# The last two pairs of products of a decoder's short convolution, multiplied with seven block products instead of eight

## The chip, the cores and the metric

The kernel runs on one core of one Trainium2 chip. The metric is the device time of one execution in microseconds (us); the time of a kernel is the median of its runs. PE is the matrix engine, DVE the vector engine, ACT the scalar engine, POOL the GpSimd engine, SP the queue engine that issues most transfers.

## The reference

One step of a hybrid decoder layer on 512 prompt tokens and 64 decode tokens (8 sequences of 8), all in float32, side by side as 576 columns:

```python
h = _rmsnorm(x, norm1_g) * (1.0 + sc1) + sh1
proj = h @ w_in
b_gate, c_gate, xa, q, k, v, ga, gb = jnp.split(proj, cuts, axis=-1)
u = c_gate * xa
uc, new_conv = _causal_conv(u, conv_buf, conv_w)
ya = (b_gate * uc) @ w_conv_out
o, k_state, v_state = attend(q, k, v, attn_sinks.reshape(N_KV_HEADS, GROUP))
yb = o @ w_attn_out
mixed = jax.nn.sigmoid(ga) * ya + jax.nn.sigmoid(gb) * yb
x = x + g1 * (mixed @ w_mix_out)
...
a, val = jnp.split(h2 @ w_up, 2, axis=-1)
ac, new_ffn = _causal_conv(a, ffn_buf, ffn_conv_w)
x = x + g2 * ((jax.nn.gelu(ac, approximate=False) * val) @ w_down)
```

`_causal_conv` is a depthwise convolution of width 3 along the tokens. The prompt attends within a window of 128, the decode tokens to a cache of 128 rows and to themselves; both have a learned sink in the softmax. The model width is 1024, with 16 query heads and 4 key heads of 64.

## The kernel before

Activations lie transposed: 128 channels on the partitions, the 576 tokens along the row. The width of 1024 is 8 blocks of 128, numbered k where they are summed over and m where they are produced. Float32 accuracy is reached with two numbers of a shorter format for each value, a high part (`hh`, `whi`) and a low part (`hl`, `wlo`, value less high part), and three passes of matmuls: high by high, high by low, low by high.

`product(w, xs)` is the plain form for one m: for 8 k, 3 passes and 2 column groups (256 and 320) one matmul each, 48 in all. After each k it calls `tick()`.

`pair_product` does two m at once by Strassen's method. Weights are seen as 2 by 2 blocks (two halves of k, two m), activations as 2 by 2 blocks (two halves of k, two halves of 288 columns), and seven block products of 4 k and 3 passes take the place of eight: 84 matmuls of 288 columns, a tick for each of 28 k steps. They accumulate in four banks X, Y, Z, W. After parts 1 and 3 ACT copies the bank to `p1` and `p5`; after part 2 DVE makes `u = Y - p1`, after part 4 `out_a0` takes X, after part 6 DVE makes `v = Y - p1`, then `out_b0(v, W)` and `out_b1(v, p5)`, after part 7 `out_a1(Z, u)`. Y is written in parts 2 and 6, X in 1 and 4, Z in 3 and 7. The sums and differences of weights that the parts need come from `pair_weights`: four additions on DVE and four high and low parts (A, B, C of 1024 columns, D of 512). `in_turn` deals them out as steps behind parts 0, 2, 3 and 4 of the pair ahead. The low parts of B and D are made by ACT and an accumulating transfer that POOL issues, those of A and C by DVE. `PairOperands` makes the sums of the activations: `sums` (DVE: `r`, `tw`), `high` (ACT: `th`, `nh`), `low` (DVE: `tl`, `nl`) and `n3`, four of them for the four pairs of k.

The order of the stage that is changed: keys, values and the first queries come first. Then a loop over the 8 m makes c and x by two plain products each (column blocks 1024 + 128 m and 2048 + 128 m of `w_in`), c copied by ACT (L1314), u = c times x by DVE (L1324, L1325), the state kept, and `conv` run: POOL puts the old state into u, ACT does the first tap, DVE the other two, into `y`. Behind it four pairs (`b_pair`, `B_PAIRS`) make b and multiply it by y, then eight pairs make the sigmoid gates, then the output projections follow. The four `PairOperands` of h are made in the loop's last four m (4 to 7), the first b pair's weights are loaded in m = 6, and their last steps run in m = 7.

The attention runs beside all this as a generator. `fill` sets a rate, `tick()` adds the rate at each k step of a product, and each whole number that is passed runs the generator to its next `yield`. While the prompt's 16 blocks run, the rate is 0.285 (`ATT_RATE`); the decode part then takes 0.35, and 0.2 once the b pairs begin. What is left over is run by `drain()` behind the b pairs. A decode half (q = 0, 1, four sequences each) is `decode_scores` (two transposes of caches, each followed by a copy `kTc`; the scores; the softmax) and `decode_values`; the values of q = 0 come after the scores of q = 1.

PE keeps the program's order throughout the stage; ACT and DVE keep it, for the instructions issued through `act` and `dve`, from the end of the loop on, and the attention's own instructions (`nc.vector`, `nc.scalar`) don't. The rest is ordered by a scheduler with a cost model. Working tiles share 57 slots (`A_BUFS`), raw weights have 4 buffers, split weights 5; banks of PE's results are two double banks (`mm`) and four single ones (`aux`).

Of the kernel before, what the change touches and what calls it, by code (L numbers as in the profile page):

```python
# [13 lines left out]
ALU = mybir.AluOpType  # L14
# [12 lines left out]
NF = FF // P  # L27
FCH = [(0, 8), (8, 16), (16, 22)]
LATE = 4
Q_TICKS = 12  # L30
CACHE_AT = 15, 16
UP_ADDING, FIRST_TICKS = "BD", 12
ATT_RATE, ADDING_FROM, B_PAIRS = 0.285, 3, ((0, 4), (1, 5), (2, 6), (3, 7))
B_ADDING, OUT_ADDING, MOD_RATE = "BD", "BCD", 12 / 130
EPS = 1e-6
NEG = -1e33
A_BUFS = 57
# [37 lines left out]
def step_kernel(ctx: ExitStack, tc: tile.TileContext, ins: dict, outs: list):  # L75
# [76 lines left out]
    def load_w(src, nk):  # L152

        raw = wp.tile([P, nk, P], F32, tag="raw", name=nm("raw"), bufs=W_BUFS)
        sync.dma_start(raw, src)
        return raw
# [222 lines left out]
        order = {0: "sums1 ah al", 2: "dh dl sums2", 3: "bh bl", 4: "ch cl"}  # L379
        return {at: (lambda names=names: [t[n]() for n in names.split()]) for at, names in order.items()}  # L380

    def pair_product(w, x, steps, out_a0, out_a1, out_b0, out_b1):

        X, Y, Z, W = (t[:, :HT] for t in (aux(), mmps(), mmps(), aux()))
        keep, uv = slot("p15"), slot("uv")
        p1, p5, u, v = keep[:, :HT], keep[:, HT:], uv[:, :HT], uv[:, HT:]

        def part(at, bank, wn, xn_, more=False):  # L390

            (hi, lo), xs = w[wn], x[xn_]
# [547 lines left out]
    ot = [wp.tile([P, 4, NT], F32, tag="oh", name=nm("o"), bufs=2) for _ in range(2)]  # L940

    def softmax(s, n, sinks, nsinks, w):

        nmx = sp.tile([P, n], F32, tag="nmx", name=nm("nmx"))
        for x in range(n // 2):
            nc.vector.tensor_reduce(
                out=nmx[:, 2 * x : 2 * x + 2], in_=s[x][:, :, :w], axis=AX.X, op=ALU.max, negate=True
            )
# [10 lines left out]
        nc.vector.tensor_tensor(out=den, in0=den, in1=es, op=ALU.add)  # L959
        nc.vector.reciprocal(out=den, in_=den)  # L960
        for x in range(n):
            nc.vector.tensor_scalar(
                out=s[x // 2][:, x % 2, :w], in0=s[x // 2][:, x % 2, :w],
                scalar1=den[:, x : x + 1], scalar2=None, op0=ALU.mult,
            )

    caches = {}

# [10 lines left out]
    def decode_scores(q, s, cV):  # L979
# [35 lines left out]
                    in1=S[hf][:, at : at + 256], op0=ALU.mult, op1=ALU.add,  # L1015
                )
        yield False
        softmax(s, 4, snks, nsnks, 256)
        yield False

    def decode_values(q, s, cV):
# [98 lines left out]
    def attention():  # L1120
# [3 lines left out]
        for n in range(19):  # L1124
# [14 lines left out]
                h4 = slice(4 * arg[0], 4 * arg[0] + 4)  # L1139
                softmax(scored[2], 4, snk[:, h4], nsnk[:, h4], 256 if arg[1] else P)  # L1140
            yield False
        filler[1] = 0.35
        waiting = None
        for n in range(3):
            s, more = [], []
# [138 lines left out]
        for t in (2 * n, 2 * n + 1):  # L1284
            queries(t)

    for m in range(NK):
        if m in (5, 6):
            src, dst = ((ins["cache_k_win"], nks), (ins["cache_v_win"], nvs))[m - 5]
            tc.keep_in_program_order(  # L1290
                nc.gpsimd.dma_start(
                    dst[:, 0:120, :].rearrange("b (x w) c -> b x (w c)", x=2),
                    src[0].rearrange("b w h d -> b w (h d)")[:, 8:128, :].rearrange(
                        "b (x w) c -> b x (w c)", x=2
                    ),
                )
            )
        ps = product(conv_w(1024 + m * P), h)
        if m == NK - 2:
            raws = [load_w(kpm(w_in, j * P), NK) for j in B_PAIRS[0]]  # L1300
            w_pair, steps = pair_weights(*raws, B_ADDING)
            steps = in_turn(steps)
        w = conv_w(2048 + m * P)
        if m == NK - 1:
            for n in (2, 3, 4):
                steps[n]()
        if m == 0:
# [8 lines left out]
            head(1)  # L1316
        if m == 1:
            head(3)
        if m >= NK - 4:
            ops[m - NK + 4].sums()  # L1320
            ops[m - NK + 4].high()
        ps = product(w, h)
        u = padded()
        nc.vector.tensor_tensor(out=u[:, 2:514], in0=pv(ps), in1=pv(c_sb), op=ALU.mult)  # L1324
# [7 lines left out]
        if m >= NK - 4:  # L1332
            ops[m - NK + 4].low()
        if m == NK - 2:
            steps[0]()
        ys[m] = y
    pinned += [act, dve]
# [10 lines left out]
    def b_pair(ma, mb, w, steps):  # L1348
# [21 lines left out]
        pair_product(w, made["op"], steps, a0, later(ta, ya), b0, later(tb, yb))  # L1370
        gate_in[ma], gate_in[mb] = ta, tb

    gate_in, w_next, w_pair = [None] * NK, {}, [w_pair]
    filler[1:2] = [0.2] if filler else []
    gate_cols = [c + m * P for c in (4608, 5632) for m in range(0, NK, 2)]
    cols = [(ma * P, mb * P) for ma, mb in B_PAIRS[1:]] + [(c, c + P) for c in gate_cols]
    raws = {}

    def raws_for(n):
# [4 lines left out]
    def weights_for(n):  # L1384

        raws_for(n + 1)
        w, t = pair_weights(*raws.pop(n), B_ADDING if n < len(B_PAIRS) - 1 else "")
        w_pair.append(w)
        return in_turn(t)

    raws_for(0)
    for n, (ma, mb) in enumerate(B_PAIRS):
        first = [{0: lambda: [op.n3() for op in ops]}] if n == 0 else []
        b_pair(ma, mb, w_pair.pop(0), merged(*first, weights_for(n)))
    state_out(NK, ncv_p[:], ncv_s[:])
    drain()
    fill(first_modulation(), MOD_RATE)
# [46 lines left out]

    for n in range(len(gate_cols)):
        if n + 1 < len(gate_cols):
            steps = weights_for(n + len(B_PAIRS))
        else:
            drain()
            w, t = pair_weights(*out_raws(1), OUT_ADDING)  # L1450
# [688 lines left out]
```

## Time and profile before

| what | value |
|---|---|
| median of 3 runs | 979.55 us (979.48 to 979.82) |
| the profiled execution | 980.01 us, its span 978.2 us |
| granted PE clock | 0.997 of full |
| busy: PE, DVE, ACT, POOL | 965.2, 687.2, 527.3, 157.8 us |
| moved by DMA | 149.34 MB, 153 GB/s in the mean |

The span is the time from the first to the last event of the profiled execution; the execution's own time has about 1.8 us around it. Busy PE counts matmuls, whose ends are modelled, so PE's figure says little alone; it is read together with what PE waited for. The loop over m with its two products ends at about 263.1 us of the span, the four b pairs follow to about 314 us.

### The profile page before, as it was taken

Reading aid. Unit: us, or ns where it says so; the run is one execution under the profiler, and the core shown is the slowest. Engines: PE = TensorE matmul, PEld = TensorE weight load, DVE = VectorE, ACT = ScalarE, POOL = GpSimd, SP = SyncE. Lnnn points to the kernel's source line nnn. Section 1 sums busy time; section 2 is a strip of 40 time slices with the busy share of each in tenths; the row PEclk is TensorE's granted clock in tenths of the full one; section 3 lists DMA queues with packets and bytes.
Section 4 is the critical chain, followed back from the end, with each engine's and each line's share of the span. In section 5 each row is a group of like instructions: output and inputs, shape, how many; then the busy total and the mean of one; then the engine's idle time right before and its main releaser. Section 6 shows DMA issues by size and latency. Waiting matters only on the chain.

```text
span 978.2 us, 18982 instructions
## 1 busy us (share of the span) xinstructions
PE 965.2 (99%) x7420; PEld 929.5 (95%) x7420; DVE 687.2 (70%) x1337; ACT 527.3 (54%) x960; POOL 157.8 (16%) x347
## 2 busy tenths in 40 slices
PE   7999999999999999999999999999999999999997
PEld 6799999999999889999899999999999999999996
DVE  5555875674868667897578687785558874578753
ACT  6365667664654434675234468662347742256553
POOL 2132222011222000011000041220013220022120
PEclk9999999999999999999999999999999999999998
DMA  9994345475366772468952444772457762557502
GB/s 309 308 264 125 94 100 124 110 207 148 77 132 173 246 230 83 123 139 215 373 190 85 131 110 99 161 193 84 104 136 164 167 166 65 131 127 174 130 9 98
DMA packets 183563, 149.34 MB, mean 153 GB/s; under 512 B 8007, under 2 KB 161966, under 8 KB 183186
## 3 DMA queue, kind: packets, MB, share of 16 engines
q1 hardware_dynamic: 169954, 108.83, 36.5%
q0 software_dynamic: 13088, 38.52, 19.5%
q8 instruction: 58, 0.95, 0.4%
q10 hardware_dynamic: 432, 0.79, 0.2%
q14 instruction: 31, 0.25, 0.1%
HBM read 109.17 MB, written 7.35 MB: 119 GB/s over the span
## 4 chain that ended last, share of the span: by engine, by line
PE 95%; DMA 2%; SPq 1%; issue 1%; DVE 0%; POOL 0%; POOLq 0%; DVEq 0%
PE mm L114 64%; PE aux L114 27%; PE aux L1208 2%; DMA ad<-in_w_ada 2%; PE aux L1107 1%; SPq L433 1%; DMA x<-in_x_prompt 0%; POOL r L114 0%; DVE yo L114 0%; POOLq L2135 0%; DVE wlo L114 0%; DVEq L2135 0%; DVE r L114 0%
## 5 line engine op out<-in xcount | busy, mean ns | idle before, releaser
L114 ACT ACTIVATE whi<-raw 128x1024 fp32r<-128x1024 f32 (+2 forms) x174 | 177.7, 1031 | 100.7 <-PE mm L114 45.8
L114 DVE TENSOR_TENSOR wlo<-raw,whi 128x1024 fp32r<-128x1024 f32 (+2 forms) x129 | 152.2, 1183 | 49.3 <-ACT whi L114 47.5
L114 PE MATMUL mm<-hh,whi 128*128 128x256 f32 (+2 forms) x448 | 104.4, 302 | 0.6 <-ACT hh L114 0.5
L114 POOL DMA_DIRECT2D wlo<-raw x45 | 39.4, 876 | 390.8 <-ACT wlo L114 221.2
L114 PE MATMUL mm<-hh,wlo 128*128 128x256 f32 (+2 forms) x448 | 100.7, 294 | 0.1
L114 PE MATMUL mm<-hl,whi 128*128 128x256 f32 (+2 forms) x448 | 99.4, 295 | 0.3 <-DVE hl L114 0.2
L114 PEld LDWEIGHTS mm<-hh,whi 128*128 128x128 f32 x448 | 74.7, 188 | 9.8 <-issue 7.8
L114 PE MATMUL mm<-th,whi 128*128 128x288 f32 x280 | 82.7, 295 | 0.0
L114 PE MATMUL mm<-tl,whi 128*128 128x288 f32 x280 | 82.7, 295 | 0.0
L114 PE MATMUL mm<-th,wlo 128*128 128x288 f32 x280 | 82.6, 295 | 0.0
L114 PEld LDWEIGHTS mm<-hh,wlo 128*128 128x128 f32 x448 | 76.4, 188 | 0.3 <-DVE wlo L114 0.3
L114 PEld LDWEIGHTS mm<-hl,whi 128*128 128x128 f32 x448 | 75.3, 188 | 1.0 <-DVE hl L114 1.0
L114 PE MATMUL mm<-fh,whi 128*128 128x256 f32 (+1 forms) x304 | 65.4, 296 | 0.0
L114 PE MATMUL mm<-fh,wlo 128*128 128x256 f32 (+1 forms) x304 | 65.0, 295 | 0.0
L114 PE MATMUL mm<-fl,whi 128*128 128x256 f32 (+1 forms) x304 | 64.8, 294 | 0.0
L114 DVE SCALAR_TENSOR_TENSOR x<-mm,modT,x 128x512 f32<-128x512 f32 (+1 forms) x29 | 19.6, 677 | 61.8 <-PE mm L114 61.8
L114 PEld LDWEIGHTS mm<-th,whi 128*128 128x128 f32 x280 | 52.7, 188 | 0.8 <-issue 0.8
L114 PEld LDWEIGHTS mm<-th,wlo 128*128 128x128 f32 x280 | 52.7, 188 | 0.0
L114 PEld LDWEIGHTS mm<-tl,whi 128*128 128x128 f32 x280 | 52.6, 188 | 0.0
L114 PEld LDWEIGHTS mm<-fh,whi 128*128 128x128 f32 x304 | 51.0, 188 | 0.1
L114 PEld LDWEIGHTS mm<-fl,whi 128*128 128x128 f32 x304 | 50.9, 188 | 0.0
L114 PEld LDWEIGHTS mm<-fh,wlo 128*128 128x128 f32 x304 | 50.7, 188 | 0.0
(357 smaller groups left out, 2864.4 us busy)
## 6 DMA issues: line engine op xcount, KB each, us to landing
raw<-in_w_in SPq DMA_DIRECT2D x52, 512.0 KB, 4.9
wlo<-raw POOLq DMA_DIRECT2D x45, 512.0 KB, 4.9
raw<-in_w_up SPq DMA_DIRECT2D x44, 512.0 KB, 3.9
ada<-in_w_ada SPq DMA_DIRECT2D x64, 256.0 KB, 5.1
ad<-in_w_ada SPq DMA_DIRECT2D x32, 256.0 KB, 5.8
raw<-in_w_down SPq DMA_DIRECT2D x16, 512.0 KB, 4.0
wl<-s POOLq DMA_DIRECT2D x25, 256.0 KB, 4.2
raw<-in_w_conv_out SPq DMA_DIRECT2D x8, 512.0 KB, 4.5
```

Source lines behind the costliest of these rows:

```text
L114: done = getattr(self.engine, name)(*args, **kwargs)
L433: return tc.keep_in_program_order(queue.dma_start(dst, src))
L1107: done = nc.tensor.matmul(O[HALF[par], :256], vt(i - nkt + 1 + kt)[:, hd * 64 : hd * 64 + 64], pts[kt][:, par * 256 : par * 256 + 256], st ...
L1208: done = nc.tensor.matmul(ps[32 * j : 32 * j + 32, :], cT[:, k, :], cols[k][j], start=(k == 1), stop=(k == NK - 2),)
```

## The change

c and x of m = 6 and 7 are made as two Strassen pairs, c in the place of the pair's first output and x in that of its second (`cx_pair`), between the loop, which now has six m (`CX = 6`), and the b pairs. The pair's `u` of the convolution is put together in halves: ACT copies c's first half, DVE makes x's and c's others and multiplies; POOL multiplies the decode columns. W takes the second half of Y's double bank (`single=1`), so the pair holds one `aux` bank and not two. Everything tied to the loop's end comes two m sooner: h's pair operands at m = 2 to 5, the loads and weights of the first pair at m = 4 and 5. The two cache copies in DRAM are issued at m = 4 and 5, where they were at 5 and 6. The weights of both new pairs use the accumulating form for B and D, as those of the b pairs do. The decode attention runs at 0.2 from its start and has two more steps in each half, between the exponentials and the division.

```diff
+CX = 6
-ATT_RATE, ADDING_FROM, B_PAIRS = 0.285, 3, ((0, 4), (1, 5), (2, 6), (3, 7))
-B_ADDING, OUT_ADDING, MOD_RATE = "BD", "BCD", 12 / 130
+ATT_RATE, ADDING_FROM, B_PAIRS = 0.285, 3, ((0, 4), (1, 5), (2, 6), (3, 7))
+CX_RATE, B_ADDING, OUT_ADDING, MOD_RATE = 0.2, "BD", "BCD", 12 / 130
...
-    def pair_product(w, x, steps, out_a0, out_a1, out_b0, out_b1):
+    def pair_product(w, x, steps, out_a0, out_a1, out_b0, out_b1, single=2):
-        X, Y, Z, W = (t[:, :HT] for t in (aux(), mmps(), mmps(), aux()))
+        X, yw, Z = aux(), mmps(), mmps()
+        W = aux() if single == 2 else yw[:, 512:]
+        X, Y, Z, W = (t[:, :HT] for t in (X, yw, Z, W))
...
-        softmax(s, 4, snks, nsnks, 256)
+        divide = softmax_exps(s, 4, snks, nsnks, 256)
+        yield False
+        yield False
+        divide()
         yield False
...
-        filler[1] = 0.35
+        filler[1] = CX_RATE
...
-    for m in range(NK):
-        if m in (5, 6):
-            src, dst = ((ins["cache_k_win"], nks), (ins["cache_v_win"], nvs))[m - 5]
+    cx_cols = [(1024 + m * P, 2048 + m * P) for m in range(CX, NK)]
+    for m in range(CX):
+        if m in (4, 5):
+            src, dst = ((ins["cache_k_win"], nks), (ins["cache_v_win"], nvs))[m - 4]
...
-        if m == NK - 2:
-            raws = [load_w(kpm(w_in, j * P), NK) for j in B_PAIRS[0]]
+        if m == CX - 2:
+            raws = [load_w(kpm(w_in, c), NK) for c in cx_cols[0]]
             w_pair, steps = pair_weights(*raws, B_ADDING)
             steps = in_turn(steps)
...
-        if m >= NK - 4:
-            ops[m - NK + 4].sums()
-            ops[m - NK + 4].high()
+        if m >= CX - 4:
+            ops[m - CX + 4].sums()
+            ops[m - CX + 4].high()
...
+    def cx_pair(m, w, steps):
+
+        c_sb, x_sb, u, n = slot("c"), slot("x"), padded(), 512 - HT
+        done = {}
+
+        def a0(ps):
+            act.copy(c_sb[:, :HT], ps)
+
+        def b0(x, y, op):
+            dve.tensor_tensor(out=x_sb[:, :HT], in0=x, in1=y, op=op)
+            dve.tensor_tensor(out=u[:, 2 : 2 + HT], in0=x_sb[:, :HT], in1=c_sb[:, :HT], op=ALU.mult)
+
+        def b1(x, y, op):
+            dve.tensor_tensor(out=x_sb[:, HT:], in0=x, in1=y, op=op)
+
+        def a1(x, y, op):
+            c = c_sb[:, HT:]
+            dve.tensor_tensor(out=c, in0=x, in1=y, op=op)
+            dve.tensor_tensor(out=u[:, 2 + HT : 514], in0=x_sb[:, HT:512], in1=c[:, :n], op=ALU.mult)
+            nc.gpsimd.tensor_tensor(
+                out=b10(u)[:, :, 2:10], in0=b8(sv(x_sb)), in1=b8(sv(c_sb)), op=ALU.mult
+            )
+
+        pair_product(w, made["op"], steps, a0, a1, b0, b1, 1)
+        keep_state(u, m)
+        ys[m] = conv(u, parT[:, 64 + m : 65 + m], parT[:, 72 + m : 73 + m], parT[:, 80 + m : 81 + m], stT[:, m, :])
...
-    cols = [(ma * P, mb * P) for ma, mb in B_PAIRS[1:]] + [(c, c + P) for c in gate_cols]
+    cols = cx_cols[1:] + [(ma * P, mb * P) for ma, mb in B_PAIRS] + [(c, c + P) for c in gate_cols]
...
     raws_for(0)
+    for n, m in enumerate(range(CX, NK)):
+        first = [{0: lambda: [op.n3() for op in ops]}] if n == 0 else []
+        cx_pair(m, w_pair.pop(0), merged(*first, weights_for(n)))
     for n, (ma, mb) in enumerate(B_PAIRS):
-        first = [{0: lambda: [op.n3() for op in ops]}] if n == 0 else []
-        b_pair(ma, mb, w_pair.pop(0), merged(*first, weights_for(n)))
+        b_pair(ma, mb, w_pair.pop(0), weights_for(n + len(cx_cols)))
```

More of the change, by code (lines that the diff above doesn't have):

```diff
@@ L942, in softmax, with softmax_exps @@
     def softmax(s, n, sinks, nsinks, w):
+        softmax_exps(s, n, sinks, nsinks, w)()
+    def softmax_exps(s, n, sinks, nsinks, w):
         nmx = sp.tile([P, n], F32, tag="nmx", name=nm("nmx"))
@@ L958, in softmax, with divide @@
         nc.scalar.activation(es, es, AF.Exp)
[L959 to L965, printed above, removed]
+        def divide():
+            nc.vector.tensor_tensor(out=den, in0=den, in1=es, op=ALU.add)
+            nc.vector.reciprocal(out=den, in_=den)
+            for x in range(n):
+                nc.vector.tensor_scalar(
+                    out=s[x // 2][:, x % 2, :w], in0=s[x // 2][:, x % 2, :w],
+                    scalar1=den[:, x : x + 1], scalar2=None, op0=ALU.mult,
+                )
+        return divide
     caches = {}
@@ L1303, in step_kernel @@
         w = conv_w(2048 + m * P)
-        if m == NK - 1:
+        if m == CX - 1:
             for n in (2, 3, 4):
@@ L1331, in step_kernel @@
             head(2)
-        if m >= NK - 4:
-            ops[m - NK + 4].low()
-        if m == NK - 2:
+        if m >= CX - 4:
+            ops[m - CX + 4].low()
+        if m == CX - 2:
             steps[0]()
@@ L1371, in b_pair @@
         gate_in[ma], gate_in[mb] = ta, tb
+    def cx_pair(m, w, steps):
[14 more added lines that the diff above has]
+                out=b10(u)[:, :, 2:10], in0=b8(sv(x_sb)), in1=b8(sv(c_sb)), op=ALU.mult
+            )
+        pair_product(w, made["op"], steps, a0, a1, b0, b1, 1)
+        keep_state(u, m)
+        ys[m] = conv(u, parT[:, 64 + m : 65 + m], parT[:, 72 + m : 73 + m], parT[:, 80 + m : 81 + m], stT[:, m, :])
     gate_in, w_next, w_pair = [None] * NK, {}, [w_pair]
-    filler[1:2] = [0.2] if filler else []
+    filler[1:2] = [CX_RATE] if filler else []
     gate_cols = [c + m * P for c in (4608, 5632) for m in range(0, NK, 2)]
-    cols = [(ma * P, mb * P) for ma, mb in B_PAIRS[1:]] + [(c, c + P) for c in gate_cols]
+    cols = cx_cols[1:] + [(ma * P, mb * P) for ma, mb in B_PAIRS] + [(c, c + P) for c in gate_cols]
     raws = {}
@@ L1386, in weights_for @@
         raws_for(n + 1)
-        w, t = pair_weights(*raws.pop(n), B_ADDING if n < len(B_PAIRS) - 1 else "")
+        w, t = pair_weights(*raws.pop(n), B_ADDING if n < len(cols) - len(gate_cols) else "")
         w_pair.append(w)
@@ L1446, in step_kernel @@
         if n + 1 < len(gate_cols):
-            steps = weights_for(n + len(B_PAIRS))
+            steps = weights_for(n + len(B_PAIRS) + len(cx_cols))
         else:
```

## The prediction

> **What bounds the kernel now.** I read the page first, then the waits of PE, then the chain of work that ended last, then windows and timelines of the stage that is changed.
>
> ```profile
> span 978.2 us, 18982 instructions
> PE 965.2 (99%) x7420; PEld 929.5 (95%) x7420; DVE 687.2 (70%) x1337; ACT 527.3 (54%) x960; POOL 157.8 (16%) x347
> ```
>
> PE is busy for 965.2 of 978.2 us. Busy PE is not yet proof that PE bounds, so I asked who PE waited for between 56 and 920 us. The answer is a heading with nothing under it:
>
> ```profile
> core 0 of [0], span 978.2 us
> engine line waited for: us in total, times, longest us
> ```
>
> Nothing is late for PE in the whole middle of the kernel. So a matmul taken out there is worth its pace in full, and every wait that the change creates on PE costs in full. The pace is read from the chain (start, length, what, how many instructions):
>
> ```profile
> 237.45 0.44 PE aux L114 x4
> ...
> 240.28 1.60 PE aux L114 x40
> ...
> 259.09 3.97 PE mm L114 x30
> 263.06 1.59 PE aux L114 x12
> ...
> 265.44 2.60 PE aux L114 x20
> ...
> 280.38 1.59 PE aux L114 x12
> 281.97 3.17 PE mm L114 x24
> 285.14 3.20 PE aux L114 x24
> 288.34 3.19 PE mm L114 x24
> ...
> 410.48 15.91 PE mm L114 x120
> ```
>
> 15.91 us for 120 matmuls of plain products is 132.6 ns each (256 and 320 columns in turn, 288 in the mean); 3.97 for 30, the end of x for m = 7, is 132.3. The second of today's pairs is the four rows from 280.38 to 291.53: 84 matmuls of 288 columns in 11.15 us, 132.7 ns each. A column costs the same in both, so the count decides.
>
> **The multiplications.** A product is 8 k by 3 passes by 2 column groups, 48 matmuls. c and x of two m are 192. A pair is 7 parts by 4 k by 3, 84; two are 168. So 24 matmuls go: 24 x 132.7 ns = 3.18 us. That is the whole gain; nothing else leaves PE, since the decode's transposes, scores (1.60 us for 40 in the row at 240.28) and values (2.60 us for the 20 that start at 265.44) only change their place. The profiled execution took 980.01 us, 0.46 over the median; its span of 978.2 is what the sum changes, and a difference carries over to the median.
>
> The Trainium skill, "TensorE: Matmul & The Clock Gate", section "Wait — 56ns, not 53.3ns?", gives back-to-back matmuls as columns divided by 2.4 GHz plus 2.5 ns; for 288 columns that is 122.5 ns, so by this estimate 24 are 2.94 us and the forecast would be 0.24 us later. The trace has 132.7 ns, and the measured pace stays in the sum.
>
> **DVE beside the pairs.** A cx pair needs u, x and c put together on DVE, and the convolution's two taps behind it; today's b pairs need ta and tb. DVE keeps program order here. This is the boundary between b pairs 2 and 3 (PE's part 7 ends at 291.53):
>
> ```profile
> 289.97 0.46 DVE L114 TENSOR_TENSOR uv<-mm,p 128x288 f32<-128x288 f32 x1 [0.29 <-PE mm L114]
> 290.46 0.45 DVE L114 TENSOR_TENSOR cy<-uv,aux 128x288 f32<-128x288 f32 x1
> ...
> 292.12 0.45 DVE L114 TENSOR_TENSOR uv<-mm,uv 128x288 f32<-128x288 f32 x1
> 292.61 0.39 DVE L114 TENSOR_TENSOR cy<-uv,y 128x224 f32<-128x224 f32 x1
> 292.92 0.81 DVE L114 TENSOR_TENSOR s<-raw,raw 128x512 f32<-128x512 f32 x1
> 293.76 0.69 DVE L114 TENSOR_TENSOR raw<-raw 128x512 f32<-128x512 f32 x1
> 294.37 1.22 DVE L114 TENSOR_TENSOR wlo<-raw,whi 128x1024 fp32r<-128x1024 f32 x1
> 295.50 0.45 DVE L114 TENSOR_TENSOR uv<-mm,p 128x288 f32<-128x288 f32 x1
> ```
>
> The row at 292.61 is the last output of pair 2; the next three belong to step 0 of pair 3; the row at 295.50 is pair 3's u, which reads Y after part 2. Y is written again by part 6, five parts after the pair's start: 291.53 + 5 x 1.59 = 299.48. u is done at 295.95, 3.5 us ahead. After a cx pair the convolution stands between 292.92 and u:
>
> ```profile
> L114 DVE SCALAR_TENSOR_TENSOR y<-pad,parT,y 128x592 f32<-128x592 f32 x16 | 13.3, 831 | 2.0 <-ACT y L114 1.9
> L114 ACT ACTIVATE y<-pad,parT 128x592 f32<-128x592 f32 x8 | 6.3, 783 | 3.3 <-DVE pad L1325 2.4 <-POOL sto L1185 1.0
> L1364 POOL TENSOR_TENSOR cy<-p,y x4: 422/514/520, 278.2 to 314.1; 128x64 f32<-128x64 f32 x4
> L1165 POOL COPY pad<-stT x8: 212/616/1806, 99.3 to 257.0; 128x16 f32<-128x16 f32 x8
> ...
> 285.47 1.06 ACT L114 ACTIVATE whi<-raw 128x1024 fp32r<-128x1024 f32 x1
> ...
> 293.17 0.40 ACT L114 COPY p<-aux 128x288 f32<-128x288 f32 x1 [3.79 <-PE aux L114]
> ```
>
> POOL's small multiply (0.51) can start with DVE's last multiply, ACT's first tap (0.78) follows, then DVE's two taps (0.83 each). DVE stands still for about 0.51 + 0.78 - 0.39 + 0.2 for two hand-overs = 1.1 us and works 1.66. So u moves by 2.8 us, and of the 3.5 us ahead 0.7 stay. In order behind the waiting tap stand step 0's sums and the split of A; who waits for those is PE's part 6, through u. If the 0.7 is used up, PE waits for what is over. On ACT, in order too, the tap holds up the next pair's split of A (1.06) and the copy p1, which frees X for part 4 at 3 x 1.59 = 4.8 us: 0.39 + 0.51 + 0.2 + 0.78 + 1.06 + 0.4 = 3.3 us, in time. ACT's load, 7.21 us in a b pair (below) with the copy of c and the tap on top, is 8.4 of 11.15.
>
> On POOL the rows say more: the copy of stT takes from 212 to 1806 ns, so a small POOL operation beside a full DVE can be 1.6 us late, and this copy is one that ACT's tap waits for, though it can be made early. The Trainium skill, "SBUF — State Buffer", section "Who interferes with whom", states that a DVE tensor_tensor with both inputs in SBUF contends with GpSimd's reads, the first to start holding the port. By that rule POOL's multiply would wait for DVE's 0.39 us one beside it, and the 0.7 us would be 0.3; the row's spread of eight to one agrees with such blocking, without showing which port.
>
> The second draw on that slack is the decode attention, which now lies beside the cx pairs:
>
> ```profile
> L1013 DVE SCALAR_TENSOR_TENSOR s<-con,aux 128x256 f32<-128x256 f32 x8 | 3.3, 473 | 4.5 <-PE aux L114 4.5
> L946 DVE TENSOR_REDUCE nmx<-s 128x2 f32<-128x512 f32 x4 | 2.5, 675 | 0.0
> L962 DVE TENSOR_SCALAR s<-s,den 128x256 f32<-128x256 f32 x8 | 2.3, 345 | 0.0
> ```
>
> Per half (q) that is 4 x 0.47 + 2 x 0.68 + 4 x 0.35 = 4.6 us, plus four tiny ones. Twenty steps at 0.2 per k step (28 to a pair) take 100 k steps, 3.6 pairs; scores, exponentials and division of q = 0 fall at k steps 15, 20 and 30 and those of q = 1 at 45, 50 and 60. So each cx pair gets about 3.3 us of it, where DVE is free:
>
> ```profile
> 214.20:230.20 16.00, 16.00 (x123) 14.45 (x121) 9.05 (x19) 7.88 (x14) 2.78 (x6) 1.00 0.60 166
> ...
> 247.60:263.06 15.46, 15.46 (x148) 14.66 (x147) 15.24 (x37) 10.10 (x22) 4.11 (x6) 1.00 0.40 90
> ...
> 280.38:291.53 11.15, 11.15 (x87) 11.15 (x86) 8.23 (x14) 7.21 (x13) 2.19 (x3) 1.00 0.58 119
> ```
>
> Behind the window's length stand PE, PEld, DVE, ACT and POOL with their instructions, then clock, DMA share and GB/s. DVE has 8.23 us of 11.15 in b pair 2. A cx pair has a0 on ACT (0.45 off DVE) and the taps (1.66), so 9.4; with the decode 12.7 us in a stretch that PE fills for 11.15 plus about 2.5 of decode matmuls (0.44 for each four cache transposes, 1.60 for scores) = 13.6. That fits with 0.9 to spare, less the 1.1 us of standing still if no decode work fills it. The window from 247.60 to 263.06 (m = 7) shows that DVE can be full, 15.24 of 15.46, and PE not wait. I take 0.5 us of waiting in all. The ends: nothing, if decode work falls into the gap; and 1.36 (two reductions) + 1.4 (four scalings) = 2.8 us if both fall ahead of u, less the 0.7, at each of the two boundaries behind cx pairs: 4.2.
>
> For the first cx pair there is a row already, since the same list (two pads, nl, tl, taps, hl, sums, split) stands ahead of the first pair now:
>
> ```profile
> 270.30 0.45 DVE L114 TENSOR_TENSOR uv<-mm,p 128x288 f32<-128x288 f32 x1
> ```
>
> It ends at 270.75, 7.7 us behind the start at 263.06; part 6 begins after 5 x 1.59 = 7.95 plus the decode matmuls among the parts. That fits by 0.25 plus two groups of transposes.
>
> **What moves sooner.** Pair operands at m = 2 to 5 instead of 4 to 7:
>
> ```profile
> L114 DVE TENSOR_TENSOR r<-hh,hl 128x576 f32<-128x576 f32 x4 | 2.8, 750 | 0.0
> L114 DVE TENSOR_TENSOR tl<-tw,th 128x576 fp32r<-128x576 f32 x3 | 2.2, 750 | 0.0
> ...
> 200.00:230.00 30.00, 30.00 (x229) 27.54 (x228) 17.86 (x44) 17.38 (x40) 4.75 (x10) 1.00 0.63 170
> 240.00:260.00 20.00, 20.00 (x210) 18.40 (x209) 15.45 (x35) 10.01 (x24) 4.11 (x6) 1.00 0.29 64
> ```
>
> Each costs DVE two r, four sums and nl of 288 columns (0.45, as u above) and tl: 1.5 + 1.8 + 0.45 + 0.75 = 4.5 us. DVE has 12 us free of the 30 from 200 to 230, and weights for the first pair (two splits of 1.22, four sums: 5.3) come there too. 4.5 + 5.3 fits in 12: hidden; without the cover each would delay the first pair by its own length. SP issues the first pair's two raw loads two m sooner, past the cache loads, and POOL the two cache copies to DRAM one m sooner, past the accumulating transfers of wlo; DMA is at 0.63 from 200 to 230, so there is room: nothing. The lost aux bank (Y and W in one mm tile) frees an aux buffer; the tile is free when b0 has read W, at 290.91 in the rows above, and needed at part 2, 1.59 behind 291.53: 2.2 us of slack: nothing.
>
> **Sum.** -3.18 + 0.5 = -2.7 us on 979.55: 976.9.
>
> **Rivals.** (1) *DVE takes the gain back* (chance 0.24): division and reductions fall ahead of u behind the cx pairs, 1.2 to 4.2 us of PE waits, time 977.6 to 980.6, about 979. For it: DVE's full window; against it: the decode's own DVE instructions aren't held in program order, so they can fill the gap, and PE's decode matmuls put part 6 off. (2) *Slots* (0.28, slower): there are 57 working slots. In the first cx pair I count h 16, operands 12, y 6, caches 8, kT, qS, con2 and V 5, the pair's keep and uv 2, c, x and pad 3, two sets of sums and their splits 6, kTc and s 4: 62. Beside today's first pair I count 57 to 59. Something must wait, on engines that keep program order, and PE, in order as well, comes to a score or a pair part whose operand isn't made. The trace shows one such wait already:
>
> ```profile
> SPq L974 <- DVE s L962: 5.2, 1, 5.2
> ```
>
> A cache load stood 5.2 us for a slot. One such wait on PE gives 979.55 - 3.18 + 5.2 = 981.6, two 986.8. It decides from 3.2 us on (no gain), from 5.1 on it reads as slower. Against it: the caches of q = 1 may come late at no cost, and at 57 to 59 today PE waits for nothing. (3) *The count does not drop* as told: ruled out by counting, unless decode steps left over run alone in the drain; 3.6 of six pairs leave none.
>
> **How the numbers follow.** A measurement of this kernel can tell about 0.2% (1.96 us) from no change. Forecast 0.48 (waits under 1.2 us, 976.4 to 977.6); DVE 0.24, nearly all within 0.2%; slots 0.28, nearly all slower. Faster 0.48, same 0.24, slower 0.28. The low end, 976.0, is no wait at all (976.4) less the 0.34 by which the runs of before lie apart; the high end, 983.0, takes in one slot wait and some 1.4 us of DVE beside it, leaving out the upper half of the slots' case. The likeliest case's own range is 976.0 to 977.6.
>
> **What would show it.** Right: PE has 24 matmuls fewer, the stage from m = 6 to the first sigmoid pair is 2.7 us shorter, the waits of PE there are under 0.7 us in all, and taps follow at once on ACT's y. Wrong by (1): PE mm waits for DVE uv in part 6 of cx pair 2 or b pair 1. Wrong by (2): PE waits for kTc, th, tl or wh, and SP, ACT or DVE before it for a slot. Wrong altogether: the shorter stage is there and a later one is longer.

## The result and the profile after

| kernel | median of its runs | profiled execution | span |
|---|---|---|---|
| before, on the same chips | 979.81 us (979.48 to 980.29, 6 runs) | 980.01 us | 978.2 us |
| after | 975.83 us (975.49 to 976.28, 6 runs) | 975.77 us | 974.0 us |

The change is a gain: the ratio is 0.9960, interval 0.9947 to 0.9973, 3.98 us less. The prediction had 976.9 and, as its low end, 976.0; the kernel is 0.17 us below that end. So the direction was right, and the range too narrow on the side where I had thought myself safe.

The page of the kernel after, its span and engines:

```profile
span 974.0 us, 18976 instructions
PE 960.2 (99%) x7396; PEld 924.6 (95%) x7396; DVE 699.9 (72%) x1359; ACT 529.8 (54%) x968; POOL 156.9 (16%) x349
```

7420 matmuls have become 7396, the 24 of the count. The waits of PE between 56 and 920 us in the kernel after are again a heading with nothing under it:

```profile
core 0 of [0], span 974.0 us
engine line waited for: us in total, times, longest us
```

So all of PE's time between those points is pace. Three rows of the chain (start, length, what) that both kernels have cut the span at the same work: the 125 matmuls that begin near 56 us, the 20 in which the next modulation's first eight stand (the first gate pair, right behind the b pairs), and the last six before the end stage. Before:

```profile
56.36 14.85 PE aux L114 x125
...
313.81 2.47 PE aux L114 x20
...
960.31 0.58 PE mm L114 x6
```

After, with the starts of the two cx pairs and of the first b pair between them:

```profile
56.22 14.85 PE aux L115 x125
...
231.12 1.80 PE aux L115 x12
...
245.12 1.59 PE aux L115 x12
...
258.95 1.59 PE aux L115 x12
...
310.50 2.46 PE aux L115 x20
...
406.97 15.80 PE mm L115 x120
...
956.05 0.58 PE mm L115 x6
```

From the first row to the second it was 257.45 us and is 254.28: 3.17 us less, and 24 matmuls at the predicted 132.7 ns are 3.18. From the second to the third it was 646.50 and is 645.55: 0.95 us less, in a stretch in which both kernels issue the same matmuls in the same order, at a granted clock of 1.00 (window 316 to 955 us of both), and in which PE waits for nothing in either. 0.14 comes before the first row. Together 4.26, against 4.2 by the spans. The middle term, 0.95, is what the prediction did not have. The plain product shows it in small: 120 matmuls that took 15.91 us (the row at 410.48 in the prediction) take 15.80.

The windows of the two cx pairs and the first b pair (length, then PE, PEld, DVE, ACT, POOL, granted clock, DMA share, GB/s):

```profile
231.12:245.12 14.00, 14.00 (x134) 13.20 (x135) 13.32 (x27) 10.55 (x22) 2.72 (x6) 1.00 0.34 68
245.12:258.95 13.83, 13.83 (x134) 13.03 (x134) 12.90 (x28) 8.79 (x18) 3.05 (x7) 1.00 0.57 135
258.95:271.96 13.01, 13.01 (x102) 12.91 (x101) 11.29 (x24) 9.19 (x20) 2.77 (x5) 1.00 0.50 121
```

DVE is at 12.90 of 13.83 us in the second, where the prediction had 12.7 of 13.6. It is nearly full, and PE does not wait. DVE's timeline behind the first cx pair shows why:

```profile
246.68 1.14 DVE L972 TENSOR_SCALAR s<-s,den 128x256 f32<-128x256 f32 x4
247.83 1.71 DVE L115 SCALAR_TENSOR_TENSOR y<-pad,parT,y 128x592 f32<-128x592 f32 x2
249.45 0.69 DVE L115 TENSOR_TENSOR s<-raw,raw 128x512 f32<-128x512 f32 x1
250.06 0.45 DVE L115 TENSOR_TENSOR uv<-mm,p 128x288 f32<-128x288 f32 x1
250.42 0.68 DVE L115 TENSOR_TENSOR raw<-raw 128x512 f32<-128x512 f32 x1
251.02 1.22 DVE L115 TENSOR_TENSOR wlo<-raw,whi 128x1024 fp32r<-128x1024 f32 x1
```

The decode's division fills the gap in which DVE waits for ACT's tap, and u (`uv`) comes ahead of the second sum and the split of step 0, not behind them.

### The profile page after: what moved, and what is told of

It reads as the page before. It is cut to its first block, busy times and chain, and to the rows that moved or that the text cites. A ratio compares the mean times of both kernels' runs of the same rounds, so it can differ in the third digit from the quotient of the medians.

```text
span 974.0 us, 18976 instructions
## 1 busy us (share of the span) xinstructions
PE 960.2 (99%) x7396; PEld 924.6 (95%) x7396; DVE 699.9 (72%) x1359; ACT 529.8 (54%) x968; POOL 156.9 (16%) x349
## 4 chain that ended last, share of the span: by engine, by line
PE 95%; DMA 2%; issue 1%; SPq 1%; DVE 0%; POOL 0%; ACT 0%; POOLq 0%; DVEq 0%
PE mm L115 64%; PE aux L115 28%; PE aux L1223 2%; PE aux L1122 1%; DMA ad<-in_w_ada 1%; SPq L437 1%; DMA x<-in_x_prompt 1%; POOL r L115 0%; ACT hh L115 0%; DVE hl L115 0%; DVE yo L115 0%; POOLq L2180 0%; DVEq L2180 0%; DVE xn L115 0%; DVE modT L115 0%
## 5 line engine op out<-in xcount | busy, mean ns | idle before, releaser
L115 DVE TENSOR_TENSOR wlo<-raw,whi 128x1024 fp32r<-128x1024 f32 (+2 forms) x133 | 157.0, 1183 | 52.3 <-ACT whi L115 50.7
L115 PE MATMUL mm<-hh,whi 128*128 128x256 f32 (+2 forms) x392 | 92.4, 302 | 0.6 <-ACT hh L115 0.6
L115 PE MATMUL mm<-hh,wlo 128*128 128x256 f32 (+2 forms) x392 | 89.4, 294 | 0.0
L115 PE MATMUL mm<-hl,whi 128*128 128x256 f32 (+2 forms) x392 | 88.1, 295 | 0.3 <-DVE hl L115 0.2
L115 PE MATMUL mm<-th,whi 128*128 128x288 f32 x296 | 87.8, 297 | 0.0
L115 PE MATMUL mm<-th,wlo 128*128 128x288 f32 x296 | 87.2, 295 | 0.0
L115 PEld LDWEIGHTS mm<-hh,whi 128*128 128x128 f32 x392 | 65.8, 188 | 9.1 <-issue 7.5
L115 PEld LDWEIGHTS mm<-hh,wlo 128*128 128x128 f32 x392 | 67.2, 188 | 0.3 <-DVE wlo L115 0.3
L115 PEld LDWEIGHTS mm<-hl,whi 128*128 128x128 f32 x392 | 66.1, 188 | 1.0 <-DVE hl L115 1.0
L115 DVE TENSOR_TENSOR raw<-raw 128x512 f32<-128x512 f32 x74 | 51.2, 692 | 2.5
```

Source lines behind the costliest of these rows:

```text
L115: done = getattr(self.engine, name)(*args, **kwargs)
```

## The experiments

**Where the 0.95 us in unchanged stages come from.** The first thought was scatter from one execution to the next, the second that the working slots, which are dealt out in another order, have an effect of their own: a tile in another place in memory is read at another pace. Both kernels were run again unchanged:

> The kernel before once more, unchanged. Two theories for the 0.8 us that the change gained beyond its 24 matmuls (3.18 us): places (the pace of a matmul depends on where its operands lie in the working slots, and the change dealt the slots anew) and scatter (the pace wanders from execution to execution). Places: the starts of its matmuls agree with those of the first profile of before within 0.1 us over the whole span, apart from a constant set in the first 40 us. Scatter: they drift by up to 0.7 us behind the b pairs, as they do between before and after. Time 979.8 +- 0.3 by both.

> The changed kernel once more, unchanged. Both: -3.9 us against before. Places: its matmul starts agree with those of its first profile within 0.1 us. Scatter: they drift by several tenths, and the gain varies between 3.2 and 4.3.

They gave 979.91 and 975.72 us. The three rows of the chain lie at 56.81, 314.25 and 960.75 before, and 56.22, 310.48 and 956.02 after: the stretches are 257.44 and 646.50, and 254.26 and 645.54, the first profiles' to 0.02 us. All that varies between executions lies ahead of 56 us. Scatter is out.

One idle slot behind the b pairs moves the tiles that come later and changes no other instruction:

```diff
+    def stand_in(n):
+        for _ in range(n):
+            nc.gpsimd.memset(slot("dum")[:, 0:2], 0.0)
...
+    stand_in(1)
```

> The kernel before with one idle slot taken and given back (a memset of 2 columns on POOL) behind the b pairs, so that tiles made later lie in other slots; every matmul, split and transfer is as before. Places: no difference up to 315 us of the span, then a drift of some tenths of a us in either direction, no new wait of PE, and a time 0.2 to 0.8 us off before. Scatter: no difference in the mean, under 0.15 us.

It took 980.17 us; the second stretch grew from 646.50 to 646.88. In the changed kernel, with one and with three:

> The changed kernel with one working slot taken and given back idle behind the last b pair, so that the tiles from there on lie in other slots; no instruction that computes is changed. Theory (places): the pace of the later matmuls depends on where their operands lie, so the starts agree with the changed kernel to 0.01 us up to about 302 us and drift by some tenths of a microsecond behind it, either way; PE's waits stay as they are; 975.3 to 976.3. Rival (the later 0.8 us come from the order of the work, not from places): starts agree to the end, 975.7 to 975.9.

> As after_slot1 with three idle slots, so another placing of the later tiles. Places: once more some tenths either way against the changed kernel from about 302 us on and another value than after_slot1, 975.2 to 976.5, PE's waits unchanged. Rival (order of the work): 975.7 to 975.9 with starts that agree to the end.

975.67 and 975.34 us; the second stretch, 645.55 without, is 645.77 with one and 645.37 with three, and PE's waits are unchanged. So places count, both ways, but these shifts are smaller than 0.95. The test that decides gives each kernel the other's places. In the last 554 tiles, from ahead of the b pairs to the end, one fixed exchange of slots turns the kernel before's places into the changed kernel's. So the slots are dealt out in another order once, at the start:

```diff
+    def first_places(order):
+        ts = [slot("dum") for _ in order]
+        for t in ts:
+            nc.gpsimd.memset(t[:, 0:2], 0.0)
+        for n in order:
+            nc.gpsimd.memset(ts[n][:, 0:2], 0.0)
...
+    first_places(
...
```

> The changed kernel with the working slots dealt out in another order at the start (57 idle tiles, each written twice with two columns by GpSimd, before the first load), so that the last 554 tiles, from ahead of the b pairs to the end, lie exactly where the kernel before has them; order and form of the matmuls are those of the changed kernel. Against the kernel before, matmul starts from 310 to 960 us: theory (places) a constant distance, to within 0.05 us, where the changed kernel drifted by 0.9 us; so about 0.8 us later than the changed kernel behind 310 us, besides what the idle tiles cost at the start. Rival (the 0.9 us come from the order of the work or from what the pairs leave behind): the drift of 0.9 us stays. The whole: 976.5 plus the start, which I put at 0 to 8 us.

> The kernel before, its slots dealt out at the start so that the last 555 tiles lie where the changed kernel has them. Theory (places): against the changed kernel a constant distance from 310 to 960 us, to within 0.05 us, and against the kernel before 0.9 us gained in that stretch with no matmul fewer. Rival: against the kernel before nothing gained in that stretch (within 0.1). The whole: 979.0 plus the start, 0 to 8 us.

The chain of the kernel before with the changed kernel's places:

```profile
315.02 2.46 PE aux L125 x20
...
411.49 15.80 PE mm L125 x120
...
960.55 0.58 PE mm L125 x6
```

The chain of the changed kernel with the places of before:

```profile
311.90 2.47 PE aux L126 x20
...
408.56 15.91 PE mm L126 x120
...
958.61 0.58 PE mm L126 x6
```

| matmuls of | places of | 20 to last six | 120 of a product |
|---|---|---|---|
| before | before | 646.50 us | 15.91 us |
| after | before | 646.71 us | 15.91 us |
| before | after | 645.53 us | 15.80 us |
| after | after | 645.55 us | 15.80 us |

The 0.95 us go with the places and not with the change. Matmul by matmul, the changed kernel with before's places keeps a constant distance to the kernel before, to 0.001 us, from 300 to 520 us; one single delay of 0.21 us near 540 us is all that differs up to 960, and is the 646.71. The whole took 978.94 us, ratio 0.9989 (0.9981 to 0.9998), and before_places 980.25: the idle tiles, and other places in the first stage, put the 125 matmuls off to 57.70 and 57.57 us, 1.48 and 1.21 later. The stage of the change stays what it was (254.20 and 257.45 us). What the change itself is worth is therefore 3.2 us; the rest of the 3.98 is luck: a dealing of slots that gives 0.95, and a few tenths either way by which executions differ ahead of 56 us.

**How much room DVE has behind a cx pair.** The prediction charged 0.5 us of waits, from a margin of 0.7 us for u. The run adds 2.5 us of DVE work at the place in question:

```diff
+        for _ in range(3):
+            dve.scalar_tensor_tensor(
+                out=y[:, :592], in0=u[:, 0:592], scalar=zero, in1=y[:, :592], op0=ALU.mult, op1=ALU.add
+            )
```

> The changed kernel with three more multiply-adds on DVE (y + 0 * u, 592 columns, 0.83 us each, 2.5 us in all) behind the taps of each cx pair, ahead of the next pair's u. By the prediction's margin of 0.7 us PE waits 1.8 us behind each of the two cx pairs, 979.3. By the trace of the changed kernel, where u is in time by about 3.5 us, PE waits for nothing, 975.5 to 976.2. If the margin lies between, PE waits for uv by what is over 2.5.

978.60 us: neither forecast, but the one "between". Its waits of PE, and u and the matmul that it releases:

```profile
PE mm L115 <- DVE uv L115: 1.1, 2, 0.8
PE aux L115 <- ACT kTc L1002: 0.3, 1, 0.3
```
```profile
252.30 0.45 DVE L115 TENSOR_TENSOR uv<-mm,p 128x288 f32<-128x288 f32 x1
```
```profile
252.80 0.40 PE L115 MATMUL mm<-nh,whi 128*128 128x288 f32 x1 [0.78 <-DVE uv L115]
```

That matmul is the first of part 5, not of part 6. In the changed kernel part 5 of the second pair begins so:

```profile
252.22 0.29 PE L115 MATMUL mm<-nh,whi 128*128 128x288 f32 x1
```

u ends there at 250.51, so the margin is 1.7 us. With the taps the first two rows of the chain lie 256.90 us apart, 2.62 more than without them. The listed waits are 1.4 of it, but they count from the modelled end of the matmul before. By the starts of the matmuls PE loses 2.3 us at the same three places: 1.05 at part 5 of the second pair, 0.73 at the scores behind it, and 0.53 at part 6 of the first b pair. Part 5 writes W, which in a cx pair is the second half of the tile whose first half u reads. To see whether that sets the deadline, W was put in a bank of its own:

```diff
-        pair_product(w, made["op"], steps, a0, a1, b0, b1, 1)
+        pair_product(w, made["op"], steps, a0, a1, b0, b1)
```

> As after_taps3 (2.5 us of extra DVE work ahead of u behind each cx pair), but with W of the cx pairs in an aux bank of its own, as the pairs of the kernel before have it, instead of the second half of Y's tile. The order of PE's instructions is the same. Theory (the deadline of u is the first write to the tile that it reads, which in a cx pair is part 5, since W shares Y's tile): with W elsewhere the deadline is part 6, about 3 us later, so PE waits for nothing behind the first cx pair and 0 to 0.3 us behind the second; 975.5 to 976.6. Rival (u is simply late, whichever bank W has): 978.6 as after_taps3, with PE waiting for uv 1.1 us in all.

978.41 us. No wait of PE for u is listed any more. Behind the first pair part 5 starts at 252.61, before u has even begun (253.06), so the deadline was W's place in Y's tile. (Behind the second pair part 6 starts at 270.06, right behind u's end at 270.01 and 0.24 us late.) But the time did not come back. PE's waits and ACT's timeline:

```profile
PE aux L115 <- ACT kTc L1002: 1.4, 1, 1.4
```
```profile
253.23 0.63 ACT L115 ACTIVATE wh<-s 128x512 fp32r<-128x512 f32 x1 [3.33 <-DVE s L115]
253.77 0.61 ACT L115 ACTIVATE wl<-s 128x512 fp32r<-128x512 f32 x1
254.29 0.56 ACT L1002 COPY kTc<-aux 128x512 f32<-128x512 f32 x1
```

Behind the same late DVE stands a second deadline: ACT waits 3.33 us for step 0's sum, its second cache copy `kTc` stands behind that wait, and the scores need the copy. My theory had one deadline and there were two.

**Whether the decode's smaller portions matter.** The old portions in the new kernel:

```diff
-        divide = softmax_exps(s, 4, snks, nsnks, 256)
-        yield False
-        yield False
-        divide()
+        softmax(s, 4, snks, nsnks, 256)
...
-        filler[1] = CX_RATE
+        filler[1] = 0.35
```

> The changed kernel with the decode attention in its old portions: the division in one piece with the exponentials, and 0.35 instead of 0.2 steps per k step, so that both halves' scores fall into the first cx pair. Theory (engine order: exponentials and divisions stand on ACT and DVE ahead of p1 and u): PE waits for p or uv inside the cx pairs, 2 to 6 us in all, 978 to 982. Rival (slack of about 3.5 us at each boundary, as the changed kernel's trace reads): PE waits under 0.3 us, 975.4 to 976.3.

981.28 us, ratio 1.0014 (1.0005 to 1.0023): the pairs with the old portions and the old rate are worth nothing (the run changes both, so it doesn't say which of the two counts). The one wait of PE, and windows around it (the clock is the third figure from the end):

```profile
PE aux L115 <- ACT kTc L1001: 2.5, 1, 2.5
```
```profile
236.00:244.00 8.00, 8.00 (x90) 7.20 (x89) 6.94 (x14) 5.13 (x12) 1.73 (x2) 1.00 0.32 59
244.00:247.00 3.00, 0.52 (x11) 0.26 (x9) 1.84 (x7) 3.00 (x9) 0.00 (x0) 1.00 0.57 112
247.72:254.55 6.83, 6.83 (x46) 5.98 (x46) 4.56 (x13) 1.08 (x5) 0.00 (x0) 0.50 0.51 153
```

The theory's time came out, but PE waited for neither p nor u: the second half's cache copies stood on ACT behind the first half's exponentials, a copy of c and a split. PE waited 2.5 us, and from 247.72 to 254.55 the granted clock was half, with matmuls of 288 columns 0.24 us apart instead of 0.13. The first stretch is 260.28 us, 6.0 more than in the changed kernel, for a wait of 2.5; by that pace (an estimate) the low clock is about 3 of it. The engine was ACT, not DVE as rival (1) had it.

The same trap with a single pair:

```diff
-CX = 6
+CX = 7
...
-        if m in (4, 5):
+        if m in (5, 6):
```

> Only m = 7 as a pair (CX = 7, cache copies at m = 5 and 6 as before). Count theory: 12 matmuls fewer, the end of the b pairs comes 1.6 us sooner than before with no wait of PE, half of what two pairs bring there (3.2). Places: the time at the end is -1.6 with up to 0.8 either way. Rival, that the decode beside the pairs brings or costs the time: not half, but nearly all of 3.2 or none.

985.96 us, ratio 1.0058 (1.0045 to 1.0070): neither forecast, but a loss. The scores fall directly ahead of the pair, so their exponentials stand on ACT ahead of p1, and the same happens at the first b pair. PE's waits, the matmul behind the first of them, and the windows after both in which the clock was low:

```profile
PE aux L115 <- ACT p L115: 4.9, 2, 2.8
```
```profile
253.34 0.40 PE L115 MATMUL aux<-hh,whi 128*128 128x288 f32 x1 [2.05 <-ACT p L115]
```
```profile
254.29:257.70 3.41, 3.41 (x16) 3.39 (x16) 3.12 (x10) 3.41 (x6) 1.40 (x2) 0.50 0.43 77
271.35:274.77 3.42, 2.96 (x12) 2.96 (x13) 3.42 (x9) 3.42 (x8) 0.86 (x1) 0.50 0.08 16
```

The first stretch is 264.25 us, 10.0 more than with two pairs: 1.6 for 12 matmuls more, 4.9 of waits, and, by the same estimate, about 3 for the low clock.

**Slots.** One line each:

```diff
-A_BUFS = 57
+A_BUFS = 55
```

and 56 in the other.

> The changed kernel with 55 working slots instead of 57. The prediction's slots rival (62 wanted in the first cx pair, so that already 57 make something wait): with 55 PE waits for an operand in the cx pairs, 5 us or more, 980 or later. Theory (the pairs need fewer slots than 57, since operands are given back part by part): PE waits for under 0.5 us, and places alone move the time, 975.0 to 976.6.

> The changed kernel with 56 working slots, one fewer. With 55 DVE stood 5.8 us for a slot and the whole took 14 us longer. Theory (57 is just enough): a wait of a few us on DVE or SP for a slot and PE waiting 1 us or more in the cx pairs, 977 to 988. Rival (56 is still enough, and the change needs 56 or fewer at once): PE waits under 0.5 us, 975.0 to 976.6, by places.

55 slots give 989.68 us, ratio 1.0100 (1.0086 to 1.0114). One wait of DVE, by the waits of DVE from 226 to 240 us, and what becomes of it on PE, by the longest group of PE's:

```profile
DVE r L115 <- DMA wl<-s: 5.8, 1, 5.8
```
```profile
PE aux L115 <- ACT kTc L1001: 5.1, 2, 4.1
```

`r` doesn't read `wl`; it comes with the end of the transfer that gives a slot back, so I read the wait as one for a slot. With 56, DVE still stands once like this, 2.24 us at 229.99, and PE does not wait at all between 56 and 920 us: the stretches are 254.49 and 646.64 us. The 978.20 us of that kernel are places (1.1 us in the second stretch) and a start 1.15 later. So 56 slots are enough for PE and 55 are not; the kernel has 57.

**More pairs.** Every further m as a pair saves 12 matmuls, 1.59 us. With three (`CX = 5`) and the prompt's attention at two rates, so that the decode scores come at different points of the pair:

```diff
-CX = 6
+CX = 5
-ATT_RATE, ADDING_FROM, B_PAIRS = 0.285, 3, ((0, 4), (1, 5), (2, 6), (3, 7))
+ATT_RATE, ADDING_FROM, B_PAIRS = 0.320, 3, ((0, 4), (1, 5), (2, 6), (3, 7))
...
-        if m in (4, 5):
+        if m in (3, 4):
```

(0.31 in the second.)

> Three m of c and x as pairs instead of two, and the prompt's attention at 0.32 instead of 0.285 steps per k step, so that the decode scores come after 48 and 54 of a pair's 84 matmuls (45 and 51 in the changed kernel). Count: 12 matmuls fewer, -1.59 us. Theory (engine order and its phase decide): exponentials and division fall where they fall in the changed kernel, PE waits for nothing, 974.2, give or take 0.5 for places. Rival (a third pair's operands and weights are too much for DVE, or slots): waits on PE of 1 to 5 us in the stretch from 190 to 280 us, 975.5 to 980.

> As cx5_320, with the prompt's attention at 0.31, so that the decode scores come after 66 and 72 of 84 matmuls and the exponentials at the boundary, ahead of the next pair's first copy p1 on ACT. Theory (phase): PE waits for p1 or u at one boundary or both, 1 to 3 us each, and where a wait is over 2 us the granted clock falls behind it; 977 to 984. Rival (phase does not matter): like cx5_320 within 0.5 us.

976.80 and 981.96 us. PE's waits in cx5_310 (the three longest of five between 56 and 920 us) show u and p1 late, as the phase theory says, and the row of the 20 comes 260.75 us behind that of the 125, 6.5 more than in the changed kernel (the five listed waits add up to 5.2):

```profile
PE mm L115 <- DVE uv L115: 1.7, 1, 1.7
PE aux L115 <- ACT p L115: 1.3, 2, 0.8
PE aux L115 <- DVE s L972: 1.2, 1, 1.2
```

Its clock stayed up behind the 1.7 us:

```profile
245.20:248.00 2.80, 2.71 (x21) 2.71 (x22) 1.33 (x3) 2.80 (x5) 1.01 (x2) 1.00 0.57 99
```

cx5_320 has only the wait for a softmax, 1.2 us near 107 us, in the prompt's attention beside a plain product, where neither of its forecasts had one. Its first stretch is 254.56 us, 1.9 more than the count gives; the listed wait is 1.2 of that. A rate of 0.325, four pairs (`CX = 4`) at 0.32, and three pairs with the old rate during m = 0 were meant to avoid it; the last of them:

```diff
     for m in range(CX):
+        if m == 1:
+            filler[1] = 0.340
```

> As cx5_320, with the prompt's attention at 0.325: the decode scores come after 39 and 45 of 84 matmuls, near the changed kernel's 45 and 51, and the prompt's softmaxes fall at other places beside the single products, where cx5_320 lost 1.5 us in one wait. Theory (only phase costs): no wait over 0.3 us on PE, 974.2 give or take 0.6 for places. Rival (a rate over 0.3 always makes DVE late for a softmax): a wait of about 1.2 us in the stretch from 60 to 240 us, 975.5 to 977.

> Four m of c and x as pairs, the prompt's attention at 0.32, decode scores after 39 and 45 of 84 matmuls of the second and third pair; the rest of the prompt's attention lies beside the first pair. 24 matmuls fewer than the changed kernel, -3.18 us. Theory (only phase costs): PE waits under 0.5 us, 972.6 give or take 0.6. Rival (operands of four pairs and the prompt's attention fill DVE at the first pair): waits of 1 to 4 us there, 974 to 978.

> As cx5_320 (three m as pairs, decode scores after 48 and 54 of 84 matmuls), but the prompt's attention at the changed kernel's 0.285 steps per k step during m = 0 and at 0.34 from m = 1 on, so that the softmax at which cx5_320 lost 1.5 us near 107 us lies as in the changed kernel. Theory (that one wait was all that cx5_320 lost): PE waits under 0.3 us, 12 matmuls fewer than the changed kernel, 974.2 give or take 0.6 for places. Rival (the faster rate makes DVE late for another softmax): one or more waits of 1 to 2.5 us before 240 us, 975.5 to 979.

981.77, 980.90 and 978.25 us. Each meets a softmax of the prompt or a score somewhere else (waits of PE of 4.9, 4.5 and 2.5 us in all), so the theories were wrong. The rivals had the kind of wait right, but only the last had the time too: cx5_325 and cx4_320 came out 3 to 5 us above their rivals' ranges, and cx4_320's longest wait (2.4 us) lies near 111 us, far ahead of its first pair. None of the faster rates tried was free of such a wait, and none of these versions beat the changed kernel.

## Why the prediction was right and where it was wrong

- *The count* was right: 24 matmuls, 3.18 us forecast, 3.17 in the stage. The estimate from the Trainium skill, "TensorE: Matmul & The Clock Gate", section "Wait — 56ns, not 53.3ns?", was 2.94; the 3.17 bear out the trace's own 132.7 ns.
- *The low end, 976.0*, was argued as "no wait at all (976.4) less the 0.34 by which the runs of before lie apart". This is the step for which the range failed: with no wait at all the sum still ends inside it. The prediction put the pace of the untouched stages at no change and gave no reason; the change deals the slots anew, and in these stages that alone gave 0.95 us. From the 979.81 us of before on the same chips, 3.17 and 0.95 lead to 975.69; 975.83 was measured. The prediction thought of a later stage that gets longer, not of one that gets shorter. Over the placings of these runs the second stretch lies between 645.16 (cx5_325) and 646.88 us (before_slot1); a bound for it of about 1 us to either side would have held the result.
- *"I take 0.5 us of waiting in all"* was wrong too: there is none. The gap was priced well: DVE's taps begin 2.7 us into the pair (247.83 less 245.12), 2.5 by the prediction's rows, and the division lies in the gap at no cost, as the prediction's lower end had it. What failed is the order on DVE behind it: "in order behind the waiting tap stand step 0's sums and the split of A", and u behind them, as it stood between b pairs 2 and 3. I had u begin 3.97 + 2.8 = 6.8 us into the pair; it began 4.94 into it (250.06 less 245.12), since the sum at 250.42 and the split at 251.02, 0.68 and 1.22 us, now follow it. A second error went the other way: the deadline is part 5, not part 6, since W shares Y's tile. The margin came out at 1.7 us, not 0.7; of the 2.5 us of extra taps that leaves 0.8, and PE waited 0.78 for u there.
- *DVE's load* was right, 12.9 of 13.8 us; *rival (1)* describes kernels close to this one (2.5 us more DVE work, or the old portions), though its engine was only half right.
- *Rival (2)* was right in its mechanism and wrong in its place. I counted 62 slots wanted in the first cx pair; 56 hold. With two fewer than the kernel has, it comes true, with a wait of 5.8 us on DVE, near the 5.2 I had priced it at, and at 14 us in the whole.
- *Moved steps*: the second cache load, which waited 5.2 us in SP, waits 2.0 there now. POOL's multiply takes 0.52 us (246.21), as before (0.51). By the Trainium skill, "SBUF — State Buffer", section "Who interferes with whom", I had considered a further 0.39 for DVE's multiply beside it. That would have counted one wait twice: three of the four rows behind the 0.51 began 0.05 us behind a DVE multiply of 0.39 us themselves. The rows agree with the rule that the first to start holds up the other. In the changed kernel DVE starts first and POOL takes 0.52; the same form takes 0.32 beside DVE instructions that read a bank of PE's results (the third row):

```profile
246.16 0.39 DVE L115 TENSOR_TENSOR pad<-x,c 128x224 f32<-128x224 f32 x1
246.21 0.52 POOL L1408 TENSOR_TENSOR pad<-x,c 128x64 f32<-128x64 f32 x1 [5.24 <-DVE c L115]
...
L1883 POOL TENSOR_TENSOR pad<-uv,p x18: 315/318/325, 629.6 to 919.6; 128x64 f32<-128x64 f32 x18
```

In after_taps3, behind the second pair, POOL starts first. It takes 0.32, and DVE's multiply 0.55 instead of 0.39:

```profile
262.39 0.32 POOL L1409 TENSOR_TENSOR pad<-x,c 128x64 f32<-128x64 f32 x1 [4.60 <-DVE c L115]
262.40 0.55 DVE L115 TENSOR_TENSOR pad<-x,c 128x224 f32<-128x224 f32 x1
```

## What to carry to other kernels

Where the waits of the bounding engine are an empty list, count what leaves it, and then give the stages that you did not touch a bound of their own: a changed allocation moves their pace, which is reproducible in each kernel and so looks like an effect of the change; exchanging the placings tells the two apart. Ask for each late result which write or copy needs it first and what stands in order behind the engine that is late, since removing one deadline may only uncover the next. And price a wait on PE at more than its listed length: 2.3 us for 1.4 in after_taps3, and 6.0 for 2.5 in after_whole, where the clock fell behind it.

## What the runs showed of the hardware that I had not expected

- The pace of one and the same stream of matmuls depends on where its operands lie: 645.53 to 646.71 us over the same stretch in the four kernels of the table, with the same order of matmuls, no wait in the list, and the granted clock at 1.00. Within a placing it repeats to 0.02 us over 646. Which property of a place does it is open; I found no simple rule.
- After PE stood still for 2.05 us or more, the granted clock was 0.50 for 3.41 us (6.83 in after_whole). There were seven such gaps: 2.05 and 2.82 us in cx7, 2.48 in after_whole, 4.12 in after_a55, 2.23 in cx5_325, 2.43 in cx4_320 and 2.51 in cx5_two_rates. After 1.71 us (cx5_310) and 1.62 (cx4_320) it stayed at 1.00; what a gap between 1.71 and 2.05 does, no run shows. The Trainium skill, "TensorE: Matmul & The Clock Gate", section "Why this matters for your kernels", warns of gaps over about 3 us; here 2.05 was enough.
- A small multiply on POOL and one on DVE that both read two working tiles held each other up, by who started first: POOL's took 0.52 us instead of 0.32, or DVE's 0.55 instead of 0.39.
